# A hand-made order for three engines, a sum made by an accumulating transfer, and one more seven-product step per chunk, in a macaron FFN layer

## The chip, the cores and the metric

The kernel runs on one core of a Trainium2 chip. The metric is the time of one execution on the device, in microseconds (us). Five engines work beside each other, each through its own queue and in the order of that queue: TensorE (PE: matmuls, and PEld, its weight loads), VectorE (DVE), ScalarE (ACT), GpSimd (POOL) and SyncE (SP). SP and POOL issue the transfers between DRAM and the on-chip memory SBUF; 16 DMA engines move them. PE writes its results into PSUM.

## The reference

One decoder layer over 256 tokens with a model width of 2048, all in float32:

```python
h = h + 0.5 * swiglu(rmsnorm(h, ffn1_norm[l]), ffn1_w_in[l], ffn1_w_out[l])
u = rmsnorm(h, mix_norm[l]) @ w_in_mix[l]
y_pool = pool_mixer(...)      # trailing-window means, a small matrix per group
y_gla = gla_mixer(...)        # chunked gated linear attention
h = h + concatenate([y_pool, y_gla]) @ w_out_mix[l]
h = h + 0.5 * swiglu(rmsnorm(h, ffn2_norm[l]), ffn2_w_in[l], ffn2_w_out[l])
return rmsnorm(h, final_norm)

def swiglu(h, w_in, w_out):
    gu = h @ w_in
    gate, up = gu[..., :D_FF], gu[..., D_FF:]     # D_FF = 5632
    return (silu(gate) * up) @ w_out
```

The two FFNs (called f and z in the names) take most of the work; the change touches them and only in passing the mixer between them.

## The kernel before

**Matmuls.** Each float32 operand is split into a high part, rounded to the type fp32r, and a low part, the rest (`split_to`, `parts_of`: ACT casts to the high part, L155; DVE subtracts for the low part, L156). One product is three matmuls, high by high, high by low and low by high (`three`, L191).

**Steps.** An FFN runs over 11 chunks of 512 hidden units. For chunk c its *first product* multiplies the 256 tokens with 1024 columns (512 of the gate, 512 of the other half), in 8 steps of 256 rows of the input; a *second product* multiplies the hidden values of two chunks with 1024 output columns, in 4 steps. A step's weights are one raw tile of 1 MB: four blocks of 128 x 512, two rows by two columns, loaded by two DMAs of 512 KB on SP's queue (`load`, L135). The tokens are two blocks as well, so a step is a 2 x 2 by 2 x 2 block product.

An S step (`s_step`, `Group.s`) does it with eight products, 24 matmuls, and needs the parts of the four blocks. A W step (`w_step`, `Group.w`) does it with seven, 21 matmuls, after Winograd: besides three of the blocks it needs four sums of blocks, which DVE makes in the raw tile (L179, three instructions over 2, 1 and 1 blocks), and their parts, so the parts of seven blocks. The left factors' sums (`s_factors`) are made once per FFN. The products of W steps that belong to more than one quarter of the result gather in PSUM tiles of their own (pw); after the last W step of a chunk `combine` adds them up (an ACT copy, L297, and four DVE sums, L298 to L301) into the two tiles add, and at the chunk's end two DVE additions (L483) bring them to the rest (ps).

A chunk's string in `KINDS` says which steps are W. From chunk 3 on it is WWWWWWSS.

**Chunk end.** Each half of the 256 tokens has its silu on ACT (L490) and its gate product on DVE (L492), then PE transposes the result in 8 small matmuls (L499), and ACT and DVE split that (L504, L505). The order of groups (`GROUPS`) puts a second product over the two chunks before in between: after chunk c's first product comes the second product of chunks c-2 and c-1 for one half of the output columns. Its result is halved on ACT (L534) and added to h in DRAM by accumulating DMAs on POOL's queue (L537). The last two second products of an FFN end in `finish`.

**Buffers.** A ring of 4 raw tiles (3, and 1 more in the FFNs), and a ring of blocks for the parts: 16, and 6 more in the FFNs, taken round and round.

**Order.** The code is written step by step; the framework's scheduler decides the order of every engine's queue from its own timing estimate, so an engine's instructions of neighbouring steps are mixed. DMAs on SP are issued in the order in which their tiles are taken.

Of the kernel before, what the change touches and what calls it, by code (L numbers as in the profile page):

```python
# [33 lines left out]
ALU = mybir.AluOpType  # L34
# [25 lines left out]
W_PAIRS = (1, 3, 4, 6, 2, 5)  # L60
CHUNKS = ("WWWWWWSS",) * 8
# [11 lines left out]
RING = 16  # L73
MORE_RAW = 1
MORE_RING = 6
WIDE = True
# [6 lines left out]
def layer(ctx: ExitStack, tc: tile.TileContext, io):  # L83
# [35 lines left out]
    raws, blocks = Ring(), Ring()  # L119
# [25 lines left out]
    def parts_of(src, runs, cw=CW):  # L145

        res = []
        for x in runs:
            i = x.start
            while i < x.stop:  # L150
                n, new = blocks.take(x.stop - i)
                hi, lo = (y[:, :, :cw] for y in new)
                for j in range(0, n, 2):
                    k = min(j + 2, n)
                    nc.scalar.copy(out=hi[:, j:k, :], in_=src[:, i + j : i + k, :])  # L155
                nc.vector.tensor_tensor(  # L156
                    out=lo, in0=src[:, i : i + n, :], in1=hi.bitcast(F32), op=ALU.subtract
                )
                res += [(hi[:, j, :], lo[:, j, :]) for j in range(n)]
                i += n  # L160
        return res

# [4 lines left out]
    def s_step(src, parts=1, runs=WIDE):  # L167

        w = load(src, parts=max(parts, 2)).rearrange("p (b c) -> p b c", c=CW)
        b = parts_of(w, SINGLES if parts == 4 else PAIRS if parts == 2 or not WIDE else ALL)  # L170
        return lambda k, n: b[n if k == 0 else 3 - n]

    def w_step(src):

        w = load(src).rearrange("p (b c) -> p b c", c=CW)
        f = dict(zip(("B11", "B22", "B21"), parts_of(w, (slice(0, 1), slice(2, 4)))))

        def less(out, x, y):
            nc.vector.tensor_tensor(out=out, in0=x, in1=y, op=ALU.subtract)  # L179


        less(w[:, 0:2, :], w[:, 1:2, :].broadcast_to([P, 2, CW]), w[:, 0:4:2, :])
        less(w[:, 2, :], w[:, 2, :], w[:, 0, :])
        less(w[:, 3, :], w[:, 3, :], w[:, 2, :])
        f.update(zip(("T1", "T3", "T2", "T4"), parts_of(w, PAIRS)))
        return f
# [6 lines left out]
    class Group:  # L193
# [35 lines left out]
        def s(self, a, block):  # L229
# [7 lines left out]
            for k in range(2):  # L237
                for t in range(NT):
                    for n in range(2):
                        self.part(a, block, t, n, k, self.bound[f"{t}{n}"] == self.n - 1 and k == 1)  # L240

# [18 lines left out]
        def w(self, a, s, b):  # L260

            if self.one is None:
# [6 lines left out]
                first = True  # L269
# [864 lines left out]
```

## Time and profile before

| | |
|---|---|
| three runs | 1703.19, 1703.42, 1704.94 us (median 1703.42) |
| span of the profiled execution | 1702.4 us |
| granted TensorE clock, mean | 0.998 |
| DMA, mean | 215 GB/s; 335.6 MB on SP's queue, 27.3 MB on POOL's |
| FFN f, mixer, FFN z, begin of their first matmul | 5.6, 702.6, 1001.0 us |
| a chunk of FFN z (first product to the next first product) | 62.1 us |

The profiled execution has no time of its own beside its span; the span, from its first to its last instruction, is 1.0 us under the median of the runs. In the rows of the profile a line number (L191) is a line of the kernel, x is a count, and a tile's name is that of the program without its number: ps_fi is the sum of FFN f's first product (input), ps_fo its second product (output), pw_fi the extra products of its W steps; zi and zo are the same for FFN z. Raw tiles and blocks taken from the FFNs' own part of the rings are called fring and zring, the others ring. In the view of the windows each row has the stretch, its length, and for PE, PEld, DVE, ACT and POOL the busy time with the number of instructions, then the granted clock, the share of DMA time and GB/s.

### The profile page before, as it was taken

To read this page: it belongs to the slowest core of one execution; us is meant where nothing else is said; L and a number is where in the kernel's file an instruction comes from. 1 tells how busy PE (TensorE), PEld (TensorE's weight loads), DVE (VectorE), ACT (ScalarE), POOL (GpSimd) and SP (SyncE) were. 2 spreads that over 40 slices of the span, in tenths; PEclk is the share of its full clock that TensorE was granted. 3 is DMA by queue.
4 is the path that set the end of the run, shared out by engine and by line. 5 is a ranking of instruction groups with operands and counts; after the bars stand their busy time and mean duration, and the time that the engine had idled before them with its cause. 6 is when DMAs were issued, how large, how long until landed. Compare 5 with 4: busy or idle time off the path is not lost.

```text
span 1702.4 us, 20984 instructions
## 1 busy us (share of the span) xinstructions
PE 1689.7 (99%) x7705; PEld 1403.1 (82%) x7705; DVE 1411.5 (83%) x1565; ACT 999.3 (59%) x1272; POOL 62.9 (4%) x70
## 2 busy tenths in 40 slices
PE   9999999999999999999999999999999999999997
PEld 7888888888888888888988888888888888888886
DVE  8779999999999996645564677999999999998974
ACT  7655666665666664563454554666656656566553
POOL 0000000000000000000000000000000000000012
PEclk9999999999999999999999999999999999999999
DMA  9856856857767776554665764676666667677781
GB/s 355 338 142 229 259 156 229 269 165 221 259 178 221 246 240 215 185 182 139 197 214 169 228 203 155 196 249 195 214 244 208 203 235 227 192 245 218 215 298 50
DMA packets 105241, 365.30 MB, mean 215 GB/s; under 512 B 11809, under 2 KB 15009, under 8 KB 105138
## 3 DMA queue, kind: packets, MB, share of 16 engines
q1 hardware_dynamic: 97026, 335.63, 58.1%
q0 software_dynamic: 7392, 27.27, 8.1%
q8 instruction: 60, 0.98, 0.2%
q10 hardware_dynamic: 720, 1.07, 0.2%
q14 instruction: 43, 0.35, 0.1%
HBM read 338.75 MB, written 25.17 MB: 214 GB/s over the span
## 4 chain that ended last, share of the span: by engine, by line
PE 91%; DVE 5%; DMA 2%; issue 1%; ACT 1%; SPq 0%; POOL 0%; POOLq 0%; ACTq 0%; DVEq 0%
PE ps_fi L191 17%; PE ps_zi L191 14%; PE ps_fo L191 14%; PE ps_zo L191 12%; PE pw_fi L191 8%; PE pw_zi L191 7%; PE ps_h L191 5%; PE ps_mp L191 3%; PE ps_mv L191 3%; DVE ring_lo L156 2%; PE ps_mg L191 2%; PE ps_mq L191 1%; DMA ring_raw<-in_ffn_w_out 1%; PE ps_w_mk L191 1%; DVE ring_raw L179 1%
## 5 line engine op out<-in xcount | busy, mean ns | idle before, releaser
L155 ACT CAST ring_hi<-ring_raw 128x1024 fp32r<-128x1024 f32 (+3 forms) x544 | 501.4, 942 | 381.6 <-DMA ring_raw<-in_ffn_w_in 79.8
L156 DVE TENSOR_TENSOR ring_lo<-ring_raw,ring_hi 128x1024 fp32r<-128x1024 f32 (+6 forms) x463 | 573.8, 1250 | 182.5 <-ACT ring_hi L155 181.4
L179 DVE TENSOR_TENSOR ring_raw<-ring_raw 128x512 f32<-128x512 f32 (+1 forms) x243 | 207.4, 862 | 0.3
L155 ACT CAST zring_hi<-ring_raw 128x1024 fp32r<-128x1024 f32 (+1 forms) x113 | 99.6, 887 | 54.5 <-DMA ring_raw<-in_ffn_w_out 11.8
L191 PE MATMUL ps_fi<-ring_lo,xT_hi 128*128 128x512 f32 x324 | 126.5, 390 | 0.5 <-DVE ring_lo L156 0.4
L191 PE MATMUL ps_fi<-ring_hi,xT_lo 128*128 128x512 f32 x324 | 125.8, 389 | 0.0
L191 PE MATMUL ps_fi<-ring_hi,xT_hi 128*128 128x512 f32 x324 | 124.2, 390 | 1.2 <-ACT ring_hi L155 1.2
L156 DVE TENSOR_TENSOR zring_lo<-ring_raw,zring_hi 128x1024 fp32r<-128x1024 f32 (+3 forms) x101 | 112.2, 1117 | 11.9 <-ACT zring_hi L155 11.8
L155 ACT CAST ring_hi<-zring_raw 128x1024 fp32r<-128x1024 f32 (+1 forms) x85 | 84.2, 991 | 48.0 <-PE ps_zi L191 22.8
L191 PE MATMUL ps_zi<-ring_lo,h_hi 128*128 128x512 f32 x288 | 112.1, 389 | 0.0
L191 PE MATMUL ps_zi<-ring_hi,h_lo 128*128 128x512 f32 x288 | 112.1, 390 | 0.0
L191 PE MATMUL ps_zi<-ring_hi,h_hi 128*128 128x512 f32 x288 | 111.3, 390 | 0.0
L156 DVE TENSOR_TENSOR ring_lo<-zring_raw,ring_hi 128x1024 fp32r<-128x1024 f32 (+2 forms) x65 | 94.2, 1451 | 7.4 <-ACT ring_hi L155 7.3
L191 PE MATMUL ps_fo<-ring_lo,fhi 128*128 128x512 f32 x240 | 93.9, 391 | 0.0
L191 PE MATMUL ps_fo<-ring_hi,flo 128*128 128x512 f32 x240 | 93.8, 391 | 0.0
L191 PE MATMUL ps_fo<-ring_hi,fhi 128*128 128x512 f32 x240 | 93.4, 391 | 0.0
L191 PE MATMUL pw_zi<-ring_hi,s_z 128*128 128x512 f32 x262 | 92.5, 389 | 0.0
L191 PE MATMUL ps_zo<-ring_lo,zhi 128*128 128x512 f32 x234 | 91.5, 391 | 0.0
L191 PE MATMUL ps_zo<-ring_hi,zlo 128*128 128x512 f32 x234 | 91.4, 391 | 0.0
L191 PE MATMUL ps_zo<-ring_hi,zhi 128*128 128x512 f32 x234 | 90.7, 390 | 0.0
L191 PE MATMUL pw_fi<-ring_hi,s_f 128*128 128x512 f32 x226 | 78.7, 389 | 0.0
L155 ACT CAST ring_hi<-fring_raw 128x512 fp32r<-128x512 f32 (+1 forms) x69 | 56.9, 832 | 33.6 <-DVE fring_raw L179 9.8
(324 smaller groups left out, 3730.5 us busy)
## 6 DMA issues: line engine op xcount, KB each, us to landing
ring_raw<-in_ffn_w_in SPq DMA_DIRECT2D x262, 512.0 KB, 5.6
ring_raw<-in_ffn_w_out SPq DMA_DIRECT2D x136, 512.0 KB, 5.2
fring_raw<-in_ffn_w_in SPq DMA_DIRECT2D x44, 512.0 KB, 5.5
zring_raw<-in_ffn_w_in SPq DMA_DIRECT2D x44, 512.0 KB, 4.3
ring_raw<-in_w_out_mix SPq DMA_DIRECT2D x32, 512.0 KB, 4.3
fring_raw<-in_ffn_w_out SPq DMA_DIRECT2D x20, 512.0 KB, 6.0
zring_raw<-in_ffn_w_out SPq DMA_DIRECT2D x20, 512.0 KB, 6.0
hd<-half_f POOLq DMA_DIRECT2D x18, 512.0 KB, 8.1
```

The source lines that it names most:

```text
L155: nc.scalar.copy(out=hi[:, j:k, :], in_=src[:, i + j : i + k, :])
L156: nc.vector.tensor_tensor(out=lo, in0=src[:, i : i + n, :], in1=hi.bitcast(F32), op=ALU.subtract)
L179: nc.vector.tensor_tensor(out=out, in0=x, in1=y, op=ALU.subtract)
L191: nc.tensor.matmul(ps, x, y, start=start and i == 0, stop=stop and i == 2, **kw)
```

## The change

1. **One more W step.** The string of chunks 3 to 10 becomes SWWWWWWW: seven W steps, and the S step comes first. A seventh left factor is made in each FFN's chunk 0.
2. **A sum by a transfer.** The blocks of a step are packed in another order, and the Winograd sums take other signs, so that the first of them is the sum of two blocks. It isn't made by DVE: a DMA of 256 KB on POOL's queue reads the second block again from DRAM and adds it onto the first in the raw tile (`accum_op`), after the load. DVE makes the three others in two instructions (L279, over 1 and 2 blocks).
3. **Order by hand.** From chunk 1 of each FFN up to its last but one second product, DVE, ACT and PE issue in the order of the code (`tc.manual_schedule`). `middle` writes that order: the preparation of a step is cut into phases (casts of its blocks, their low parts, the sums, casts and low parts of the sums), each taken as far ahead as blocks are free; the matmuls of a step come in two units; the chunk's additions and gates follow one unit after the chunk's last, its transposes two units later.
4. **Blocks.** The ring of parts becomes 15 blocks and 6 more, given out by `Blocks`: in `middle` 9 of them in runs of three for the blocks of W steps, 12 for all else, the longest unused first.

The core of the diff:

```diff
-W_PAIRS = (1, 3, 4, 6, 2, 5)
-CHUNKS = ("WWWWWWSS",) * 8
+W_PAIRS = (1, 3, 4, 6, 2, 5, 0)
+CHUNKS = ("SWWWWWWW",) * 8
-RING = 16
+RING = 15
+GATE_AT = 1
+TURN_AT = 2
+T_BLOCKS = 12
+STRIDE = {"t": 2, "b": 3}
+IN_ORDER = {mybir.EngineType.DVE, mybir.EngineType.Activation, mybir.EngineType.PE}
...
-        less(w[:, 0:2, :], w[:, 1:2, :].broadcast_to([P, 2, CW]), w[:, 0:4:2, :])
-        less(w[:, 2, :], w[:, 2, :], w[:, 0, :])
-        less(w[:, 3, :], w[:, 3, :], w[:, 2, :])
...
+        def need(self, phase):
+            w = self.kind == "W"
+            return {"hi_b": ("b", 3) if w else ("t", 4), "hi_t": ("t", 4 if w else 0)}.get(phase)
...
+            w = load(self.src).rearrange("p (b c) -> p b c", c=CW)
+            self.raw = w
+            self.parts = {"b": w[:, 1:4, :], "u": w[:, 0:4:2, :], "t": w[:, 1:4:2, :]}
...
+            if self.kind == "W":
+                nc.gpsimd.dma_start(
+                    out=self.raw[:, 0, :], in_=self.src[:, CW : 2 * CW], accum_op=ALU.add
+                )
...
+            tt(w[:, 2, :], w[:, 0, :], w[:, 2, :], ALU.subtract)
+            tt(w[:, 1:4:2, :], w[:, 1:4:2, :], w[:, 2:3, :].broadcast_to([P, 2, CW]), ALU.subtract)
...
-            nc.vector.tensor_tensor(out=c[:, 1, :], in0=p75[:, 1, :], in1=u2, op=ALU.add)
+            nc.vector.tensor_tensor(out=c[:, 1, :], in0=p75[:, 1, :], in1=u2, op=ALU.subtract)
...
+            for k in range(-1, len(steps)):
+                phases += [("hi_b", k + 1), ("lo_b", k), ("sums", k), ("hi_t", k), ("lo_t", k)]
...
+            def prepare(upto):
+                nonlocal at
+                while at < len(phases):
+                    phase, k = phases[at]
+                    need = steps[k].need(phase)
+                    if need and need[1] > blocks.room(need[0]):
+                        break
+                    getattr(steps[k], phase)()
+                    at += 1
+                assert at > upto
...
+        opening(0)
+        with tc.manual_schedule(engines=IN_ORDER):
+            grp = middle(GROUPS[1:-1])
...
-        b = np.stack([b[:, :, :, 0, 0], b[:, :, :, 0, 1], b[:, :, :, 1, 1], b[:, :, :, 1, 0]], 3)
+        b = np.stack([b[:, :, :, 0, 1], b[:, :, :, 0, 0], b[:, :, :, 1, 1], b[:, :, :, 1, 0]], 3)
```

Three places show the new order. First VectorE's queue within a run of W steps of FFN f, before (L156 is a low part, L179 a difference of blocks):

```order
L179 TENSOR_TENSOR ring_raw<-ring_raw 128x1024
L156 TENSOR_TENSOR ring_lo<-ring_raw,ring_hi 128x1024
L179 TENSOR_TENSOR fring_raw<-fring_raw 128x1024
L156 TENSOR_TENSOR ring_lo<-ring_raw,ring_hi 128x1024 x2
L179 TENSOR_TENSOR ring_raw<-ring_raw 128x512
L156 TENSOR_TENSOR ring_lo<-ring_raw,ring_hi 128x1024 x2
L179 TENSOR_TENSOR ring_raw<-ring_raw 128x512 x2
```

And of the change (L220 is a low part, L279 a difference), two W steps:

```order
L220 TENSOR_TENSOR fring_lo<-fring_raw,fring_hi 128x1536
L279 TENSOR_TENSOR fring_raw<-fring_raw 128x512
L279 TENSOR_TENSOR fring_raw<-fring_raw 128x2x512
L220 TENSOR_TENSOR ring_lo<-fring_raw,ring_hi 128x1024 x2
L220 TENSOR_TENSOR fring_lo<-ring_raw,fring_hi 128x1536
L279 TENSOR_TENSOR ring_raw<-ring_raw 128x512
L279 TENSOR_TENSOR ring_raw<-ring_raw 128x2x512
L220 TENSOR_TENSOR ring_lo<-ring_raw,ring_hi 128x1024 x2
```

Steps that were mixed now follow one another whole, with each difference right behind what it waits for. Second, VectorE's queue at the end of chunk 4 of FFN f, of the change (fi in the names is the first product; L440 to L443 are the four sums of `combine`, L628 the two additions, L637 the gates, L654 the transposed chunk's low parts):

```order
L442 TENSOR_TENSOR add_fi_1_1985<-pw_fi_1_1771,add_fi_1_1985 128x512
L443 TENSOR_TENSOR add_fi_1_1985<-pw_fi_1_1771,add_fi_1_1985 128x512
L220 TENSOR_TENSOR ring_lo<-fring_raw,ring_hi 128x2048
L628 TENSOR_TENSOR ps_fi_0_1740<-ps_fi_0_1740,add_fi_0_1984 128x1024
L628 TENSOR_TENSOR ps_fi_1_1741<-ps_fi_1_1741,add_fi_1_1985 128x1024
L637 SCALAR_TENSOR_TENSOR fa_0_2014<-ps_fi_0_1740,rx_r,fs_0_2012 128x512
L637 SCALAR_TENSOR_TENSOR fa_1_2018<-ps_fi_1_1741,rx_r,fs_1_2016 128x512
L220 TENSOR_TENSOR ring_lo<-ring_raw,ring_hi 128x2048
L654 TENSOR_TENSOR flo_2059<-ftp_2049,fhi_2058 128x4x128 x2
L220 TENSOR_TENSOR ring_lo<-ring_raw,ring_hi 128x2048 x2
```

Before, some ten other instructions of later steps stood among these; now one low part stands between the sums and the additions, and nothing between additions and gates. Third, TensorE's queue at the same chunk end, of the change (ps_fo is the second product that follows chunk 4, ftp the transposed chunk):

```order
L303 MATMUL ps_fo_2_1_1992<-ring_lo,fhi_1216 128x512
L303 MATMUL ps_fo_2_1_1992<-ring_hi,flo_1217 128x512
L648 MATMUL ftp_2049<-ident,fa_0_2014 128x128 x4
L648 MATMUL ftp_2049<-ident,fa_1_2018 128x128 x4
L303 MATMUL ps_fo_2_0_1991<-ring_hi,fhi_1216 128x512
L303 MATMUL ps_fo_2_0_1991<-ring_lo,fhi_1216 128x512
```

The first product of chunk 4 has 171 matmuls where it had 174, and the eight transposes stand together behind 36 matmuls of the second product; before, the two halves stood apart, four behind 48 and four behind 52. On POOL's queue the 126 accumulating transfers into raw tiles stand in the order of their steps; those of a chunk's first four W steps are ahead of the two transfers that put the second product before them away.

330 lines of the change are left out of this document (237 added, 93 removed).

## The prediction

> **What bounds the kernel now.** The page first: its busy times, and the slices of VectorE.
>
> ```profile
> span 1702.4 us, 20984 instructions
> PE 1689.7 (99%) x7705; PEld 1403.1 (82%) x7705; DVE 1411.5 (83%) x1565; ACT 999.3 (59%) x1272; POOL 62.9 (4%) x70
> DVE  8779999999999996645564677999999999998974
> ```
>
> TensorE (PE) is busy 99% of the span, but VectorE (DVE) stands at nine tenths or more in the FFN stages, so both have to be followed. Second, the view of the waits, for PE alone:
>
> ```profile
> PE idle L575 <- DVE zeros L570: 1.2, 1, 1.2
> PE ps_fi L191 <- ACT ring_hi L155: 1.2, 2, 0.8
> PE ps_fi L191 <- DVE ring_lo L156: 0.4, 2, 0.2
> ```
>
> 2.8 us of waits in all, at the start and once later. A busy PE may still be a slow one, so third, its order of time within a run of seven-product steps, and two windows:
>
> ```profile
> 299.64 0.39 PE L191 MATMUL pw_fi<-ring_hi,xT_hi 128*128 128x512 f32 x1
> ...
> 311.88 0.39 PE L191 MATMUL pw_fi<-ring_lo,s_f 128*128 128x512 f32 x1
> ```
>
> ```profile
> 1161.88:1201.32 39.44, 39.44 (x175) 32.66 (x174) 35.20 (x36) 24.63 (x28) 0.85 (x1) 1.00 0.77 230
> 1223.98:1286.15 62.17, 62.17 (x280) 51.47 (x278) 59.61 (x62) 38.85 (x47) 1.71 (x2) 1.00 0.69 220
> ```
>
> Between the two rows quoted lie 54 starts, so a matmul starts every 12.24 / 54 = 0.2267 us, though its row says 0.39 (its result is late by the difference). The first window is one chunk's first product: 174 matmuls in 39.44 us, again 0.2267. So PE runs back to back, and a matmul that goes is 0.2267 us, if it stays fed. The second window is a whole chunk: 62.17 us, of which DVE works 59.61. The other engine is 96% full there.
>
> **What the change takes from PE.** The order shows 174 matmuls becoming 171 in chunks 3 to 10 of both FFNs (one eight-product step of 24 becomes one of 21); all other counts stay. 16 x 3 = 48 matmuls x 0.2267 = **10.9 us**. A chunk has 171 + 96 matmuls and 8 transposes: 62.17 - 0.68 = 61.5 us.
>
> **What it does to DVE.** The groups by form and the spacing of DVE's and ACT's own instructions:
>
> ```profile
> L155 ACT CAST ring_hi<-ring_raw 128x1024 fp32r<-128x1024 f32 x403 | 415.7, 1050 | 254.5 <-DVE ring_raw L179 27.3 <-PE ps_fi L191 26.9 <-DMA ring_raw<-in_ffn_w_out 26.4
> L156 DVE TENSOR_TENSOR ring_lo<-ring_raw,ring_hi 128x1024 fp32r<-128x1024 f32 x256 | 310.1, 1221 | 106.6 <-ACT ring_hi L155 105.9
> L156 DVE TENSOR_TENSOR ring_lo<-ring_raw,ring_hi 128x2048 fp32r<-128x2048 f32 x66 | 151.1, 2291 | 36.7 <-ACT ring_hi L155 36.7
> L179 DVE TENSOR_TENSOR ring_raw<-ring_raw 128x512 f32<-128x512 f32 x162 | 110.5, 684 | 0.2
> L179 DVE TENSOR_TENSOR ring_raw<-ring_raw 128x1024 f32<-128x1024 f32 x81 | 98.6, 1218 | 0.1
> L156 DVE TENSOR_TENSOR ring_lo<-ring_raw,ring_hi 128x1536 fp32r<-128x1536 f32 x15 | 26.3, 1750 | 6.8 <-ACT ring_hi L155 6.8
> L483 DVE TENSOR_TENSOR ps_fi<-ps_fi,add_fi 128x1024 f32<-128x1024 f32 x18 | 22.1, 1225 | 0.0
> L492 DVE SCALAR_TENSOR_TENSOR fa<-ps_fi,rx_r,fs 128x512 f32<-128x512 f32 x22 | 16.3, 743 | 0.0
> L490 ACT ACTIVATE fs<-ps_fi,rx_r 128x512 f32<-128x512 f32 x22 | 15.0, 686 | 13.4 <-DVE ps_fi L483 11.5 <-PE ps_fi L191 1.7
> ```
>
> ```profile
> 1174.54 1.21 DVE L156 TENSOR_TENSOR ring_lo<-ring_raw,ring_hi 128x1024 fp32r<-128x1024 f32 x1
> 1175.67 1.21 DVE L156 TENSOR_TENSOR zring_lo<-ring_raw,zring_hi 128x1024 fp32r<-128x1024 f32 x1
> ```
>
> ```profile
> 1174.64 1.05 ACT L155 CAST ring_hi<-zring_raw 128x1024 fp32r<-128x1024 f32 x1
> 1175.60 0.61 ACT L155 CAST ring_hi<-ring_raw 128x512 fp32r<-128x512 f32 x1
> ```
>
> ```profile
> 49.49 0.29 DVE L385 TENSOR_TENSOR sf_f<-sf_f,sa_f 128x128 f32<-128x128 f32 x1
> 49.81 0.29 DVE L385 TENSOR_TENSOR sf_f<-sa_f,sf_f 128x128 f32<-128x128 f32 x1
> ```
>
> Independent neighbours on DVE start 1.13 apart where one lasts 1.21: the next one starts 0.08 early. ACT's casts start 0.09 early. A neighbour that needs the other's result starts 0.03 after its end (49.49 + 0.29 to 49.81). So 512, 1024, 1536 and 2048 columns occupy DVE for 0.60, 1.14, 1.67 and 2.21 us, and a dependent instruction sees them after 0.71, 1.25, 1.78 and 2.32.
>
> A seven-product step before: lower parts of 1, 2, 2 and 2 blocks, differences of 2, 1 and 1: 0.60 + 3 x 1.14 + 1.14 + 2 x 0.60 = 6.36 us. After: 1.67 + 2 x 1.14 for the lower parts, 0.60 + 1.14 for the differences: 5.69. A chunk before: 6 x 6.36 + 6 x 2.21; after: 7 x 5.69 + 5 x 2.21. That is 51.4 against 50.9, beside the same chunk end. So the accumulating transfer pays for the seventh step: DVE's share of a chunk stays about the same, (59.61 - 0.5) / 61.5 = 96%. By shares PE remains the bound.
>
> **What the order by hand does.** Shares hide that DVE, ACT and PE now each follow one fixed order. Before, six steps with seven products come first and two with eight last, so that the four L298-L301 sums have 48 matmuls of cover before the chunk's end; the transposes follow 20 to 55 matmuls after it. Now the chunk ends with its last seven-product step, the sums, two additions and two gates come behind it, and the transposes stand after exactly 36 matmuls. I walk the longest chain. Casts of step k+1's three blocks stand on ACT ahead of step k's second casts, and need the blocks of step k-2. So from the moment PE is done with the first 9 matmuls of the chunk's first seven-product step:
>
> - casts for the fourth step (0.19 for PE's late result, 0.96 + 0.53), then the third step's cast (1.08) and two lower parts (2 x 1.14): 5.0 us
> - steps four to seven: 1.78 + 0.71 + 1.25 + 1.08 + 1.14 = 5.96 each (the cast waits for the second difference, the last lower part for the cast): 23.8
> - the next step's lower part in halves (2.28), the four sums (2.62, two of them waiting for the one before), another lower part (2.21), two additions (1.14 + 1.25), the second activation (0.72) and gate (0.77): 11.0
>
> Sum 39.9 us. PE has in the same stretch 12 + 6 x 21 + 36 = 174 matmuls and four transposes (0.35, a chunk's eight taking some 0.7): 39.4 + 0.35 = 39.8 us. **It is a tie**, short by 0.1, and forty intervals read to 0.01 make that uncertain by some 0.3. Where the chain is longer than PE's work, PE waits at the transposes by the difference, once in each of 16 chunks. Below nothing it cannot go: PE has no idle time to give back but the 2.8 us. I take 0.2 us a chunk, 3 us; the ends are 0 and 0.5 (8 us).
>
> **The accumulating transfers.** 126 of 256 KB are added, on POOL's queue, each behind its step's load and ahead of the first difference. What stands for them:
>
> ```profile
> ring_raw<-in_ffn_w_in SPq DMA_DIRECT2D x262, 512.0 KB, 5.6
> hd<-half_f POOLq DMA_DIRECT2D x18, 512.0 KB, 8.1
> q1 hardware_dynamic: 97026, 335.63, 58.1%
> q0 software_dynamic: 7392, 27.27, 8.1%
> ```
>
> ```profile
> L537 POOL DMA_DIRECT2D hd<-half_f x18: 853/862/1006, 107.7 to 607.5; - x18
> DMA to landing us min/median/max: 5.4/7.9/11.3
> ```
>
> The accumulating transfers of before (512 KB into DRAM) land in 5.4 to 11.3 us, 7.9 in the median. At half the size I take 6, from 4 to 8. When is one late? A chunk has 4 raw tiles, so a step's load waits for the lower parts of the step four ahead. Within a run that is 3 x 5.96 + 1.78 = 19.7 us before the difference, against 5.6 + 6. The tight one is the chunk's first seven-product step, whose raw tile is freed by the second step of the product before. The walk begins 138 matmuls, 31.3 us, before the chunk's end; 28.9 us later, 2.4 before that end, DVE takes up the halves (2.28), the sums (2.62) and that second lower part (2.32): free 4.8 us after the end. Additions and gates bring DVE to 8.4, then come a lower part (2.21), the transposed chunk's two lower parts with a wait for ACT (1.9), two lower parts (4.4) and the step's own (1.78): its difference is due at 18.7. Of the 13.9 us between, the load takes 5.6: a landing of the sum up to **8.3 us** costs nothing. The second such step has the same room. Behind the accumulate on POOL's queue stand the two put-away transfers of the group, needed a chunk later. Transfer time: bytes on the software queue cost 8.1% / 27.27 MB against 58.1% / 335.63 MB, 1.7 times as much; seven of 0.26 MB add some 9.3 us of 16 engines to a chunk's 0.69 x 62.2 = 43: 0.85 of the time. Loads will land later, but most have 5 us of room.
>
> POOL writes these transfers' descriptors beside a full DVE:
>
> ```profile
> 1163.40 0.85 POOL L537 DMA_DIRECT2D hd<-half_z  x1 [1.87 <-ACT half_z L534]
> ...
> 1163.94 1.22 DVE L179 TENSOR_TENSOR zring_raw<-zring_raw 128x1024 f32<-128x1024 f32 x1
> ```
>
> Neither is longer than its group's mean, so I charge nothing. The Trainium skill (SBUF — State Buffer, "Summary: rules for kernel authors") warns against hiding such a transfer under a DVE instruction, since DVE in its two-port modes locks the descriptor writer out; by that rule sums would land late, as in the rival below. The same page of the Trainium skill ("Who interferes with whom") has no two-port mode for this DVE instruction, and the rows agree. The Trainium skill's fit for one such transfer (DMA: Bandwidth & Descriptors, "Anatomy of one DMA") would give, as an estimate, 2.6 us for 256 KB; by it no sum would ever be late.
>
> **Other edits**, at nothing: a seventh set of left factors in the opening chunk, where DVE's slices stand at 7 to 9 tenths and PE has its work ahead; a ring of 15 blocks instead of 16, in stages where DVE is at 4 to 6 tenths; new signs in the sums. If the cover fails, each is under 1 us, once per FFN.
>
> **The sum.** 1702.4 - 10.9 + 3 = 1694.5 us of span. The median of the three runs, 1703.42, lies 1.0 above the span; with that, **1695.5 us**.
>
> **Rivals.**
> - *The chain is longer than I read.* 0.5 to 1 us in each of 16 chunks: 8 to 16 us back, 1700.5 to 1708.5. For it: the tie, and DVE at 96%. Against: every interval is from rows. Chance 0.18.
> - *The sum lands late* (slower). From a landing of 8.3 us on, each further microsecond moves the whole chain behind it; the gain of 0.68 a chunk is gone at 9.0. At 10.5 us it costs 2.2 x 16 = 35: 1703.4 - 10.9 + 35 = 1727.5; at the 11.3 of the slowest row, 1740.5. For it: the row's upper half, and more traffic. Against: half the bytes, and no write to DRAM. Chance 0.17.
> - *It doesn't feed less at all*: no stall anywhere, 1692.5. It is within the forecast's own spread.
>
> **How the numbers follow.** Forecast (stalls of 0 to 0.5 us a chunk: 1692 to 1700.5) 0.65; longer chain 0.18; late sums 0.17. The range runs from 1691.5 to 1710, over the first two, leaving the last out. A measurement here tells 0.2%, 3.4 us, from no change: faster (below 1700) 0.64, within (to 1706.8) 0.15, slower 0.21.
>
> **What would show it.** PE's waits: under 10 us in all, on DVE at the transposes, is the forecast; 1 us at each chunk's transposes is the first rival; DVE waiting on the accumulating transfer at the first difference of a chunk, and PE behind it, the second. The chunk's length should be 61.5 to 62.0 us, matmuls 0.2267 apart, 48 fewer of them, DMA near 0.85. A landing over 8.3 us, or DVE intervals longer than read beside the added transfers, would make me wrong.

## The result, and the profile after

The changed kernel takes **1724.79 us** (median of four runs, 1723.97 to 1726.89), the kernel before 1703.48 beside it: a ratio of 1.0126, with an interval of 1.0112 to 1.0141. It is 1.3% slower. The forecast was 1695.5, 0.5% faster. First the head of the page of after:

```profile
span 1725.1 us, 21190 instructions
PE 1686.3 (98%) x7657; PEld 1394.0 (81%) x7657; DVE 1428.5 (83%) x1353; ACT 1011.7 (59%) x1231; POOL 174.6 (10%) x196
```

TensorE has its 48 matmuls less (7705 to 7657) and VectorE's share has not changed. So the work came out as planned and the time is in waits. TensorE's waits of after (the engine's line, whom it waited for, us in all, times, the longest):

```profile
PE ps_zo L303 <- DVE add_zi L440: 9.6, 8, 1.7
PE ps_fo L303 <- DVE add_fi L440: 9.0, 8, 1.3
PE pw_zi L303 <- DVE ring_lo L220: 2.5, 4, 1.2
...
PE pw_fi L303 <- DVE ring_lo L220: 1.8, 4, 0.8
PE pw_zi L303 <- DVE zlo L654: 1.6, 1, 1.6
```

Before, all waits together were 2.8 us. Now the first matmul of the second product (ps_fo, ps_zo) waits in each of the 16 late chunks for L440, the first of the four sums that close the seven-product steps: 18.6 us. It doesn't read that sum. It writes the PSUM tile that the sum is the last to read: with two sets of two PSUM tiles used in turn, a second product accumulates where the extra products (pw) of the first product before it stood. One such place, first on TensorE, then on VectorE (start, duration, and in brackets the wait):

```profile
526.13 0.39 PE L303 MATMUL ps_fi<-ring_hi,xT_lo 128*128 128x512 f32 x1
527.79 0.50 PE L303 MATMUL ps_fo<-ring_hi,fhi 128*128 128x512 f32 x1 [1.27 <-DVE add_fi L440]
528.13 0.39 PE L303 MATMUL ps_fo<-ring_lo,fhi 128*128 128x512 f32 x1
```

```profile
522.45 4.69 DVE L220 TENSOR_TENSOR ring_lo<-ring_raw,ring_hi 128x1024 fp32r<-128x1024 f32 x4
527.06 0.68 DVE L440 TENSOR_TENSOR add_fi<-pw_fi,add_fi 128x512 f32<-128x512 f32 x1
```

The chunk's last matmul starts at 526.13, the next could start at 526.36, and L440 ends at 527.74: it stands behind four lower parts, two of the chunk's last seven-product step and two of the second product's first step. TensorE loses more than the 1.27 us that are put down to the wait: it starts 1.43 late, and its next start follows after 0.34 us instead of 0.23, some 1.54 in all.

A second thing shows on VectorE: it waits for the accumulating transfers. The row of its waits:

```profile
DVE ring_raw L279 <- DMA ring_raw<-in_ffn_w_in: 18.4, 11, 2.6
```

One such place in the order of time, on VectorE, then on SyncE and POOL, which issue the load and the sum:

```profile
472.01 2.28 DVE L220 TENSOR_TENSOR ring_lo<-ring_raw,ring_hi 128x2048 fp32r<-128x2048 f32 x1
...
486.67 1.75 DVE L220 TENSOR_TENSOR fring_lo<-ring_raw,fring_hi 128x1536 fp32r<-128x1536 f32 x1
490.27 1.95 DVE L279 TENSOR_TENSOR ring_raw<-ring_raw 128x512 f32<-128x512 f32 x2 [1.86 <-DMA ring_raw<-in_ffn_w_in]
```

```profile
474.36 7.12 SPq L185 DMA_DIRECT2D ring_raw<-in_ffn_w_in  x6
```

```profile
481.05 0.86 POOL L265 DMA_DIRECT2D ring_raw<-in_ffn_w_in  x1 [7.11 <-DVE ring_lo L220]
```

This is a chunk's second seven-product step. Its raw tile comes free at 474.29, with the first row, a lower part of the second product's third step. The load is issued at 474.36 (the first of three in that row), the sum at 481.05, and by VectorE's start the sum has landed at some 490.24, 9.2 us after its issue; VectorE was ready for it at 488.41. (The bracket of POOL's row names the lower part that freed the tile. That had ended long before; in the code the sum stands behind its load, so the load is the likelier last.) Eleven of the 16 late chunks have such a wait, of 0.76 to 2.56 us, all at this step, with the sum issued 8.6 to 9.9 us before VectorE's start. At the end of these chunks TensorE waits 1.00 to 1.65 us for L440, in the other five 0.89 or 0.90 and once 1.17. So the late sums add to a wait that is there without them. Over all 126 such transfers, by the view of their line, the landing is this:

```profile
DMA to landing us min/median/max: 4.1/6.9/13.5
```

One chunk from end to end, and its VectorE work beside it (window, length, busy us of PE, PEld, DVE, ACT and POOL, granted clock, DMA share):

```profile
486.86:550.62 63.76, 62.04 (x276) 50.78 (x275) 60.33 (x52) 39.51 (x46) 7.89 (x9) 1.00 0.84 244
```

The DMA share of 0.84 is as forecast (0.85). VectorE's 60.3 us are 1.2 more than the forecast's 59.1 (59.61 less 0.5), and the chunk takes 63.8 us where 61.5 to 62.0 were forecast.

### The profile page after: what moved, and what is told of

Its sections match the earlier page's. It is cut to its first block, busy times and chain, and to the rows that moved or that the text cites. A ratio compares the mean times of both kernels' runs of the same rounds, so it can differ in the third digit from the quotient of the medians.

```text
span 1725.1 us, 21190 instructions
## 1 busy us (share of the span) xinstructions
PE 1686.3 (98%) x7657; PEld 1394.0 (81%) x7657; DVE 1428.5 (83%) x1353; ACT 1011.7 (59%) x1231; POOL 174.6 (10%) x196
## 5 line engine op out<-in xcount | busy, mean ns | idle before, releaser
L217 ACT CAST ring_hi<-ring_raw 128x1024 fp32r<-128x1024 f32 (+3 forms) x558 | 552.4, 1014 | 379.8 <-issue 78.3
L220 DVE TENSOR_TENSOR ring_lo<-ring_raw,ring_hi 128x1024 fp32r<-128x1024 f32 (+5 forms) x443 | 633.7, 1446 | 156.2 <-ACT ring_hi L217 153.6
L279 DVE TENSOR_TENSOR ring_raw<-ring_raw 128x512 f32<-128x512 f32 (+1 forms) x178 | 170.6, 959 | 24.1 <-DMA ring_raw<-in_ffn_w_in 18.4
L303 PE MATMUL ps_fo<-ring_hi,fhi 128*128 128x512 f32 x352 | 138.8, 395 | 9.0 <-DVE add_fi L440 9.0
L265 POOL DMA_DIRECT2D ring_raw<-in_ffn_w_in x89 | 77.1, 866 | 695.8 <-DMA ring_raw<-in_ffn_w_in 349.7
L303 PE MATMUL ps_zo<-ring_hi,zhi 128*128 128x512 f32 x344 | 135.6, 395 | 9.6 <-DVE add_zi L440 9.6
L303 PE MATMUL ps_fo<-ring_hi,flo 128*128 128x512 f32 x352 | 137.2, 390 | 0.0
L303 PE MATMUL pw_fi<-ring_hi,s_f 128*128 128x512 f32 x366 | 122.8, 389 | 0.0
L217 ACT CAST ring_hi<-zring_raw 128x1024 fp32r<-128x1024 f32 x82 | 80.2, 1003 | 38.8 <-DVE zring_raw L279 23.4
L220 DVE TENSOR_TENSOR ring_lo<-zring_raw,ring_hi 128x1024 fp32r<-128x1024 f32 (+2 forms) x60 | 91.8, 1539 | 6.3 <-ACT ring_hi L217 6.2
L217 ACT CAST ring_hi<-fring_raw 128x1024 fp32r<-128x1024 f32 x72 | 71.5, 1015 | 35.2 <-issue 13.4
L220 DVE TENSOR_TENSOR ring_lo<-fring_raw,ring_hi 128x1024 fp32r<-128x1024 f32 (+2 forms) x54 | 81.4, 1518 | 12.2 <-ACT ring_hi L217 11.7
```

The source lines that it names most:

```text
L217: nc.scalar.copy(out=hi[:, j:k, :], in_=src[:, j:k, :])
L220: nc.vector.tensor_tensor(out=lo, in0=src, in1=hi.bitcast(F32), op=ALU.subtract)
L265: nc.gpsimd.dma_start(out=self.raw[:, 0, :], in_=self.src[:, CW : 2 * CW], accum_op=ALU.add)
L279: nc.vector.tensor_tensor(out=out, in0=x, in1=y, op=op)
L303: nc.tensor.matmul(ps, x, y, start=start and i == 0, stop=stop and i == 2, **kw)
```

## The experiments

All times are medians, each ratio is to the kernel before on the same chip, whose medians there were 1702.96 to 1703.60 us.

| run | us | ratio to before, interval |
|---|---|---|
| eight-product step last (s_last) | 1706.72 | 1.0021, 1.0012 to 1.0031 |
| four sums ahead of two lower parts (sums_first) | 1764.20 | 1.0354, 1.0339 to 1.0369 |
| no accumulating transfers (no_sum) | 1713.92 | 1.0059, 1.0044 to 1.0074 |
| six seven-product steps (six_w) | 1704.70 | 1.0008, 0.9998 to 1.0018 |
| s_last, lower part in halves, one step moved (best_a) | 1705.73 | 1.0013, 1.0005 to 1.0022 |
| only the first sum ahead (sums_split) | 1783.39 | 1.0463, 1.0447 to 1.0479 |
| s_last, VectorE makes the sum (dve_sum_s) | 1773.97 | 1.0412, 1.0398 to 1.0427 |
| before with seven such steps (before7) | 1806.38 | 1.0605, 1.0589 to 1.0621 |
| ScalarE frees the tile (act_frees) | 1722.44 | 1.0110, 1.0095 to 1.0124 |
| best_a, one copy earlier (best_b) | 1703.80 | 1.0004, 0.9995 to 1.0013 |
| s_last without transfers (no_sum_s) | 1705.71 | 1.0012, 1.0003 to 1.0022 |
| best_b, shorter chain (best_c) | 1693.95 | 0.9950, 0.9937 to 0.9962 |
| changed kernel, shorter chain (chain_short) | 1718.67 | 1.0100, 1.0078 to 1.0121 |
| no transfers, ScalarE frees the tile (tile_no_sum) | 1704.80 | 1.0008, 0.9999 to 1.0017 |

### The eight-product step last

```diff
-CHUNKS = ("SWWWWWWW",) * 8
+CHUNKS = ("WWWWWWWS",) * 8
```

> The eight-product step of chunks 3 to 10 stands last in the chunk (WWWWWWWS) instead of first; nothing else changes, so matmuls, vector work and transfers keep their numbers. Theory (TensorE waits at the second product's first matmul for the PSUM tile that the first of the four sums at L440 frees, and the last seven-product step at the chunk's end leaves no matmuls to cover that): 24 matmuls, 5.4 us, now stand between; the 16 waits on L440 (18.6 us of idle time) go, the waits on the seventh step's lower parts (4.3 us) stay or double, and the time is 1700 to 1706 us. Rival (VectorE's chain as a whole is too long, or the accumulating sums land late): the waits only move, to the seventh step's lower parts or to the transposes, 15 us or more of them remain, and the time is 1715 to 1726.

1706.7 us, 18 less than the changed kernel with the same work, just above what the theory gave. TensorE's waits:

```profile
PE ps_zi L303 <- DVE ring_lo L220: 2.5, 8, 0.4
PE ps_fi L303 <- DVE ring_lo L220: 2.4, 8, 0.4
PE pw_zi L303 <- DVE zlo L654: 1.6, 1, 1.6
```

No wait on L440 is left. But 16 small ones have come, 0.3 us each, on the lower part of the eight-product step: VectorE comes out of the seven steps a little late here too. So the place of that step is worth 18 us, though this run can't say whether it is the tile or something that comes with it.

### Six seven-product steps in the new order

```diff
-CHUNKS = ("SWWWWWWW",) * 8
+CHUNKS = ("WWWWWWSS",) * 8
```

> All of the change but the seventh seven-product step: chunks are WWWWWWSS as before, with the accumulating transfers and the order by hand. 48 matmuls come back (10.9 us). Theory: 48 matmuls (10.9 us) stand between the four sums and the second product, and the chain through six steps is shorter than TensorE's work, so TensorE waits under 5 us in all; 1702 to 1706 us, the time of the kernel before. Rival (the order by hand or the 126 transfers cost by themselves): 1710 to 1725, with waits of TensorE over 10 us.

1704.7: the theory. TensorE's waits are 4.7 us in all, and the ratio's interval holds 1. So the order by hand and the transfers (110 with six such steps, not the 126 of the expectation) cost nothing measurable by themselves; what the changed kernel loses comes with the seventh step and its place.

### The four sums ahead of the next lower parts

```diff
-                    prepare(place["lo_t" if i and steps[k].kind == "W" else "lo_b", k])
+                    prepare(
+                        place["lo_t" if i and steps[k].kind == "W" else "lo_b", k],
+                        not (steps[k].kind == "W" and steps[k + 1].kind == "S"),
+                    )
```

(The new argument stops `prepare` at the phase that is asked for, so the next step's lower parts are written behind L443, and two of ScalarE's casts behind its copy at L439.)

> The order of chunks stays SWWWWWWW; on VectorE the four sums at L440 to L443 are moved ahead of the two half lower parts of the second product's first step (2.3 us). Theory (the PSUM wait is real, but VectorE is also late with everything else at this place): the waits on L440 go, and TensorE waits instead for the lower parts behind the sums, 1.5 to 2.2 us a chunk; 1722 to 1737 us. Rival (only the place of the sums in VectorE's order was wrong): TensorE does not wait there at all, 1702 to 1707.

1764.2, beyond both. The direction is the theory's, the size is not:

```profile
PE ps_zo L303 <- DVE ring_lo L220: 19.4, 8, 2.8
PE ps_fo L303 <- DVE ring_lo L220: 19.0, 8, 2.4
```

The waits on L440 are gone, and TensorE waits 2.4 us in each chunk for the half lower parts that now stand behind four sums of 0.7. VectorE has nothing to spare there: what is moved ahead of one wait is paid at the next. Part of the size is another thing. Behind the stop that ends at 541.78 the granted clock (the last but two of the row) was 0.52 for 3.5 us:

```profile
541.78:545.25 3.47, 3.47 (x8) 2.76 (x9) 3.47 (x3) 0.00 (x0) 0.00 (x0) 0.52 0.60 209
```

TensorE's matmuls start 0.43 us apart there, not 0.23. Behind an equally long stop, which ends at 607.43, the clock was 1.00. The two kinds come about in turn, and chunks of the first take 65.7 us, of the second 64.1. So this time is not the price of VectorE's order alone. The second try in this direction moved only the first sum ahead:

```diff
             nc.vector.tensor_tensor(out=u2, in0=p16[:, 1, :], in1=c[:, 0, :], op=ALU.add)
+
+        def combine_rest(self):
...
+                    if rest:
+                        rest.pop()()
```

> The order of chunks is SWWWWWWW; on VectorE only the first of the four sums stands ahead of the two half lower parts of the second product's first step, the other three behind them. Theory (TensorE waits for that one sum, since it alone frees the first PSUM tile, and the first half lower part can be ready 0.7 us later): the waits on the first sum go, those on the half lower parts stay under 0.5 us a chunk; 1702 to 1712 us. Rival (VectorE's whole chain is the bound in this order, as the 1764 us with all four sums ahead suggest): TensorE waits at the lower parts or at the transposes instead, over 1720.

1783.4, with 47.8 us of waits on lower parts of the second product. The time says little, since the edit also moved the next 2048-column lower part behind the additions and gates. TensorE's order of time takes the waits apart, here at one chunk's end:

```profile
545.63 0.50 PE L303 MATMUL ps_fo<-ring_lo,fhi 128*128 128x512 f32 x1 [0.27 <-DVE ring_lo L220]
...
554.67 0.50 PE L303 MATMUL ps_fo<-ring_lo,fhi 128*128 128x512 f32 x1 [2.70 <-DVE ring_lo L220]
```

The wait on the first sum is gone, the half lower part costs 0.27 us, as the theory had it, and the last sum (L452, at 548.69) 0.26. The 2.70 are for the 2048-column lower part that the edit moved, which ends at 554.62. So the rows bear out what the theory said of the first sum and the half lower parts; what this order would take without the other move was not run.

### Without the accumulating transfers

```diff
-            if self.kind == "W":
-                nc.gpsimd.dma_start(
-                    out=self.raw[:, 0, :], in_=self.src[:, CW : 2 * CW], accum_op=ALU.add
-                )
```

> The changed kernel without its 126 accumulating transfers: the sum that they make is left out of the computation, nothing else changes. Theory (the order of VectorE against the PSUM tiles costs the time): the 16 waits on L440 stay near 1 us each; VectorE loses its 18 us of waits on these transfers, of which TensorE gets back less than half; 1712 to 1724 us. Rival (the sums land late and push the whole chain): the waits of TensorE on L440 and on lower parts fall below 6 us in all, 1694 to 1703.

1713.9, 10.9 below the changed kernel, in the theory's range. TensorE's waits:

```profile
PE ps_zo L299 <- DVE add_zi L436: 7.8, 8, 1.6
PE ps_fo L299 <- DVE add_fi L436: 7.1, 8, 0.9
```

The waits on the first sum (L436 here) stay, 14.9 us in 16 chunks, 0.88 to 0.90 in all but the last, as in the changed kernel's chunks without a late sum; and those on the seventh step's lower parts are gone. So the transfers cost the changed kernel some 11 us, more than the "less than half" of VectorE's 18 us that the theory allowed; and the wait at the first sum is there without any late transfer. The same edit where the eight-product step is last:

> The kernel with the eight-product step last, without its 126 accumulating transfers: the sum that they make is left out of the computation. It gives the price of the transfers where the PSUM tile is covered. Theory (there VectorE runs back to back through the seven steps, and the sums land in time): 1702 to 1706.5 us, at most 4 us below the kernel with them. Rival (late landings or the slower loads cost as much here as the 11 us that they cost in the changed kernel): 1694 to 1698.

1705.7 against 1706.7: 1 us, within what the runs can tell. There (in s_last) VectorE waited for a sum only three times, 1.7 us in all, with the 16 DMA engines as full (0.87 in a chunk). So the added traffic by itself is not what costs the 11 us. Late sums are thus a matter of that order too: with four raw tiles a load takes over the tile of the step four ahead. With the eight-product step first that is, for the second seven-product step, the second product's third step; with it last it is the second product's second, whose lower part VectorE makes ahead of the additions and gates. (That this is what brings the sums in time follows from the order and was not tried by itself.)

### ScalarE frees the PSUM tile

```diff
             nc.scalar.copy(out=c[:, 0, :], in_=p16[:, 0, :])
-            nc.vector.tensor_tensor(out=u2, in0=p16[:, 1, :], in1=c[:, 0, :], op=ALU.add)
+            nc.scalar.copy(out=u2, in_=p16[:, 1, :])
+            nc.vector.tensor_tensor(out=u2, in0=u2, in1=c[:, 0, :], op=ALU.add)
```

> The changed kernel (SWWWWWWW) with one edit: ScalarE copies the second half of the PSUM tile too, 512 columns, 0.57 us, so that the first of the four sums reads two copies in SBUF and the tile is free when ScalarE is done, not when VectorE has worked through the four lower parts ahead of that sum. VectorE's order and work stay. Theory (that tile is what TensorE waits for): the 16 waits on the first sum become waits on ScalarE's copy of 0.3 us or less; since VectorE is no earlier, part of the gain comes back as waits on the second tile's sums or on lower parts; 1708 to 1718 us. Rival (VectorE's chain is the bound of the whole chunk, the tile only the place where it shows): all of it comes back, 1720 to 1727.

1722.4, the rival. The first sum frees nothing any more and TensorE doesn't wait for it, yet only 2.4 us are won by the medians, with the two kernels' runs overlapping (1718.8 to 1724.8 against 1724.0 to 1726.9):

```profile
PE pw_zi L303 <- DVE ring_lo L220: 5.3, 7, 1.1
PE pw_fi L303 <- DVE ring_lo L220: 3.4, 7, 0.8
PE ps_zo L303 <- DVE add_zi L444: 3.3, 8, 1.0
PE ps_fo L303 <- DVE add_fi L444: 2.7, 8, 0.4
```

The time came back as waits on the seventh step's lower parts and on L444, the last sum, which frees the second tile. Both edits together:

> The changed kernel without its accumulating transfers (that sum is left out of the computation) and with ScalarE's second copy, so that ScalarE frees the first PSUM tile: the two edits together that gave 1713.9 (no transfers) and 1722.4 us (the copy) alone. Theory (two causes: VectorE enters the chain late by the late sums, and the tile waits for VectorE's place; with the sums gone the seventh step's lower parts are in time, so that freeing the tile now pays): the waits on the first sum, 0.89 us in each chunk, shrink to some 0.3 us on the second tile's last sum; 1703 to 1709 us. Rival (VectorE's chain is the bound in any case): the waits come back elsewhere, 1711 to 1715.

1704.8, the theory. With the sums out of the way freeing the tile is worth 9.1 us (1713.9 to 1704.8); with them in, 2.4. TensorE's waits on the last sum (L440 here) remain, 4.8 us in 16 chunks:

```profile
PE ps_zo L299 <- DVE add_zi L440: 2.7, 8, 0.8
PE ps_fo L299 <- DVE add_fi L440: 2.1, 8, 0.3
```

So there are two causes in a row: in most chunks a late sum makes VectorE enter the last steps late, and even a punctual VectorE reaches the first sum 0.9 us after TensorE wants its tile.

### The price of the seventh step without the transfer

The kernel before with WWWWWWWS, its own order and its own differences:

```diff
-W_PAIRS = (1, 3, 4, 6, 2, 5)
-CHUNKS = ("WWWWWWSS",) * 8
+W_PAIRS = (1, 3, 4, 6, 2, 5, 0)
+CHUNKS = ("WWWWWWWS",) * 8
-RING = 16
+RING = 15
```

> The kernel before with only the seventh seven-product step (WWWWWWWS), its own order of instructions and its own differences on VectorE, and a ring of 15 blocks instead of 16 to make room for the seventh set of left factors. Theory (a seven-product step costs VectorE 6.36 us without the transfer, so a chunk's VectorE work is 59.6 + 4.2 = 63.8 us against 61.5 of TensorE): about 2 us a chunk over, 1720 to 1745 us. Rival (the seventh step is to be had without the transfer and the order by hand): 1691 to 1700.

1806.4: the theory's direction at more than three times its size. In a window of 66 us VectorE has only 58.5 us of work, so the sum of its instructions, on which the expectation rested, doesn't give the time here; TensorE's waits are spread over VectorE, ScalarE and five tiles, and were not followed further.

```profile
500.00:566.00 66.00, 61.05 (x254) 47.30 (x253) 58.53 (x64) 36.43 (x45) 1.73 (x2) 0.97 0.66 199
```

And s_last without the transfers and with VectorE making the sum:

```diff
+            tt(w[:, 0, :], w[:, 0, :], w[:, 1, :], ALU.add)
             tt(w[:, 2, :], w[:, 0, :], w[:, 2, :], ALU.subtract)
```

> The kernel with the eight-product step last, the sum of each seven-product step made by VectorE (one more 512-column addition, 0.70 us, ahead of the first difference) instead of the accumulating transfer. Theory (VectorE's chain through seven such steps ties with TensorE's work, so that each addition lengthens it): 7 x 0.6 to 0.7 us a chunk, 16 chunks, less what is idle now: 1750 to 1785 us. Rival (VectorE has room, the transfer was not needed): 1700 to 1715.

1774.0, the theory: 67 us above s_last, 4.2 per chunk, for seven additions. The transfer does pay for the seventh step.

### Toward a better order, and the chain itself

From s_last on, the next wait each time:

```diff
-                        (Step(kind, w_in[g, kp]), a_of(kp), kp if kind == "W" else None)
-                        for kind, kp in pairs_of(g)
+                        (
+                            Step(kind, w_in[g, kp], kind == "S" and i == 7 and g > 2),
+                            a_of(kp), kp if kind == "W" else None,
+                        )
+                        for i, (kind, kp) in enumerate(pairs_of(g))
...
-    "z": ("SSSSSSSS", "SWSWWWSS", "WWSWWWSS") + CHUNKS,
+    "z": ("SSSSSSSS", "SSWWWWSS", "WWSWWWSS") + CHUNKS,
```

> The kernel with the eight-product step last, with two more edits: the lower part of that last step is made in two halves (in chunks 3 to 10), and the second chunk of the second FFN has its first seven-product step one place later (SSWWWWSS instead of SWSWWWSS). Theory (what the kernel with the eight-product step last still loses is its 16 waits on that lower part, gaps of some 0.45 us each, and the one wait on the transposed chunk's lower part, 1.8 us): both go, 1706.7 - 7.2 - 1.8 = 1697.7, say 1696 to 1700 us, below the kernel before. Rival (VectorE is late with everything behind): the waits move to the transposes or to the next lower parts, 1703 to 1708.

1705.7, the rival: 1 us won, within what the runs can tell. The 16 waits went, and TensorE waited for ScalarE's put-away copy instead, at the other end of the same PSUM tile's life:

```profile
PE pw_zi L303 <- ACT half_z L682: 3.0, 6, 0.6
PE pw_fi L303 <- ACT half_f L682: 2.9, 6, 0.6
```

Then that copy was moved ahead of two casts (`prepare` gets the same argument as above):

```diff
+                        i > 0 or behind is None,
```

> The kernel with the eight-product step last, its lower part in halves and the one step moved in the second FFN's second chunk, with one more edit: ScalarE's put-away copy of the second product's first row tile stands ahead of the two casts that wait for TensorE, instead of behind them. There TensorE waited 0.25 to 0.62 us in 12 of 16 chunks (the first PSUM tile of the next chunk's extra products is the one that this copy reads). Theory (a chunk has 61.5 us of TensorE work and VectorE some 60.3, so with both waits on PSUM tiles covered TensorE is the bound): these 12 gaps of 0.6 us go, 1705.7 - 7 = 1698.7, say 1697 to 1701 us. Rival (VectorE's chain from the first seven-product step to the last eight-product one is longer than TensorE's work by some 0.4 us a chunk): the wait comes back at the next place, 1703 to 1707.

1703.8, the rival again, and no different from before. The waits moved a third time, to VectorE's lower parts of the seventh step:

```profile
PE pw_zi L303 <- DVE ring_lo L220: 3.5, 8, 0.8
PE pw_fi L303 <- DVE ring_lo L220: 2.9, 7, 0.4
```

Three places in turn with the same loss: not a place but the chain through them is too long. So the next edit touched neither tile nor place, only the chain. The next step's three-block lower part goes between a step's two differences, so that no instruction waits for the result of the one just ahead:

```diff
+                ahead = 0 <= k < len(steps) - 1 and steps[k].kind == steps[k + 1].kind == "W"
-                phases += [("hi_b", k + 1), ("lo_b", k), ("sums", k), ("hi_t", k), ("lo_t", k)]
+                phases += [("hi_b", k + 1), ("lo_b", k), ("sum1", k)]
+                phases += [("lo_b", k + 1)] if ahead else []
+                phases += [("sum2", k), ("hi_t", k), ("lo_t", k)]
```

> The last kernel (eight-product step last, three edits on orders) with VectorE's order within a run of seven-product steps changed: the next step's lower part of three blocks stands between a step's two differences instead of behind its other lower parts. Same work; two starts per step that waited for the result of the instruction just ahead no longer do (0.12 us each by the rows of before). The pitch of such a step on VectorE falls from 6.05 to some 5.82 us, 0.9 us or more over the four steps of the chain that ends at the seventh step's lower parts, where TensorE waited 15 times by some 0.44 us (gaps of 0.62). Theory (that chain is what TensorE waits for): these waits go, 1703.8 - 9 = 1694.8, say 1693 to 1698 us. Rival (the wait comes back at another place, or the step's own lower parts, 1.67 us later now, come too late): 1701 to 1706.

1693.95, the theory, 0.5% below the kernel before. VectorE's order of time in best_b, then in best_c, one step each:

```profile
504.29 1.95 DVE L279 TENSOR_TENSOR fring_raw<-fring_raw 128x512 f32<-128x512 f32 x2
...
510.36 1.95 DVE L279 TENSOR_TENSOR ring_raw<-ring_raw 128x512 f32<-128x512 f32 x2
```

```profile
486.55 0.68 DVE L285 TENSOR_TENSOR ring_raw<-ring_raw 128x512 f32<-128x512 f32 x1
487.15 1.75 DVE L220 TENSOR_TENSOR fring_lo<-ring_raw,fring_hi 128x1536 fp32r<-128x1536 f32 x1
488.82 1.22 DVE L285 TENSOR_TENSOR ring_raw<-ring_raw 128x1024 f32<-128x1024 f32 x1
489.96 2.48 DVE L220 TENSOR_TENSOR ring_lo<-ring_raw,ring_hi 128x1024 fp32r<-128x1024 f32 x2
492.36 0.69 DVE L285 TENSOR_TENSOR ring_raw<-ring_raw 128x512 f32<-128x512 f32 x1
```

A step takes 6.07 us in the one and 5.81 in the other: 0.26 for two starts that no longer wait. TensorE's waits are then:

```profile
PE ztp L656 <- DVE za L645: 2.1, 2, 1.9
PE idle L812 <- DVE zeros L807: 1.2, 1, 1.2
PE ps_fi L311 <- ACT ring_hi L217: 0.7, 2, 0.4
PE ps_fi L311 <- DVE ring_lo L220: 0.2, 1, 0.2
```

None is left in the late chunks. The same edit alone on the changed kernel:

> The changed kernel (SWWWWWWW) with the same shortened order within the runs of seven-product steps and nothing else. VectorE's work, the PSUM tiles and the transfers are as in the changed kernel. Theory (the chain on VectorE through the seven steps, entered late where a sum lands late, decides; the PSUM tile is only the first place where it meets TensorE): 0.9 to 1.4 us of each chunk's 1.2 us wait on the first sum and 0.3 us on lower parts come back; 1703 to 1713 us. Rival (the place of the sums behind four lower parts decides): 1718 to 1726.

1718.7 (1715.2 to 1724.6): 6 us won by the medians, though the runs overlap; that is less than the theory had, and at the low end of the rival's range. The waits on the first sum (L448 here) fall from 18.6 to 9.6 us, and VectorE still waits for late sums:

```profile
PE ps_zo L311 <- DVE add_zi L448: 5.0, 8, 1.4
PE ps_fo L311 <- DVE add_fi L448: 4.6, 8, 0.9
```

```profile
DVE ring_raw L285 <- DMA ring_raw<-in_ffn_w_in: 13.9, 12, 1.6
```

The profiled execution (1716.7 us, one of the faster) shows where the theory holds. From each chunk's first transpose to the next, the 16 late chunks take 1000.2 us in all, 1014.3 in the changed kernel's and 982.9 in best_c's: 14 us won and 17 still lost. But the first two such stretches of the second FFN take 104.6 us where they took 100.3; the wait on the transposed chunk's lower part there is 3.2 us instead of 1.6. So in that order of chunks the chain's length is a part of the loss, not the whole.

## Why the prediction was wrong, point by point

- **TensorE's saving** (48 matmuls, 10.9 us) was right: 7705 to 7657, and best_c, where the waits of the late chunks are gone, is 9.6 us under the kernel before.
- **VectorE's share** (about the same, since the transfer pays for the seventh step) was right in the main; dve_sum_s shows the price without it. But 60.3 us in a chunk are 1.2 more than its sum gave. That sum let every instruction start 0.08 us before the end of the one ahead, and the two differences of a step, in the fixed order, cannot. In best_c, with the same work and these waits gone, a chunk has 59.4.
- **The walk is the step that failed.** It compared VectorE's chain with TensorE's work at one place, the transposes, 36 matmuls into the second product, and took 0.2 us a chunk there. It never asked what the second product's first matmul waits for, and so put the wait for the PSUM tile at nothing. By its own numbers the chain is late there: 28.9 + 2.28 + 0.71 = 31.9 us to the end of the first sum, where TensorE has 138 matmuls, 31.3 us. That is 0.6 us a chunk at the PSUM tile. The 36 matmuls on which the walk counted are not cover for it, they stand behind it. In no_sum the walk can be followed, from the cast that waits for TensorE to the first sum:

```profile
1236.68 1.05 ACT L217 CAST zring_hi<-ring_raw 128x1024 fp32r<-128x1024 f32 x1 [3.10 <-PE pw_zi L299]
1265.76 2.35 DVE L220 TENSOR_TENSOR ring_lo<-ring_raw,ring_hi 128x1024 fp32r<-128x1024 f32 x2
1268.03 0.68 DVE L436 TENSOR_TENSOR add_zi<-pw_zi,add_zi 128x512 f32<-128x512 f32 x1
```

  From that cast to the halves at 1265.76 are 29.1 us, where the walk has 28.7 (28.9 without its first 0.19); the sum ends at 1268.71, and TensorE, whose last matmul before started at 1267.49, could have gone on at 1267.72.
- **The pitch** of a step was read as 5.96 us and is 6.07 (the rows of best_b); four of them make 0.4 us. With the 0.6 this is 1.0 a chunk, as in the rows above; the waits put down to it without the transfers are 14.9 us in 16 chunks, 0.93.
- **The late sums** were a rival (1727.5, chance 0.17), put aside because a landing up to 8.3 us was to cost nothing, the load taking 5.6 of 13.9 us, with "the same room" at the second step. In the case above the sum was issued 6.7 us after the load, and landed 9.2 us later: 15.9 us, where VectorE needed it after 14.1. It was late by 1.8. The rival's mechanism was right, at the second such step rather than the first, at 11 us for the whole kernel rather than 35. Landings were taken as 6 us. They were 6.9 in the median of all 126, but 8.6 to 9.9 in the 11 places where VectorE waited, with the 16 DMA engines 0.93 full in the case above: a busy place, which the median doesn't show, and a slower load. The Trainium skill's fit for one transfer on this queue (DMA: Bandwidth & Descriptors, "Anatomy of one DMA"), 2.6 us as an estimate for this size, does not hold for these sums beside this kernel's loads: the shortest landing was 4.1.
- **Issue cost on POOL** at nothing held: VectorE's commonest group, by form, takes 1224 ns in the mean, 1221 before.

```profile
L220 DVE TENSOR_TENSOR ring_lo<-ring_raw,ring_hi 128x1024 fp32r<-128x1024 f32 x300 | 363.1, 1224 | 93.9 <-ACT ring_hi L217 91.5
```

- **Other edits at nothing** weren't tried one by one; six_w has them all, at 1704.7. What the prediction didn't walk at all is the order by hand outside the late chunks: the second FFN's second chunk has one wait on the transposed chunk's lower part (L654, 1.6 us), in the changed kernel, in s_last and in six_w, and none before.
- **The sum**: the forecast without its 3 us of stalls was 1692.5, and the changed kernel is 32.3 us above that. Of these 10.9 are the transfers (no_sum), 9.1 more the tile (tile_no_sum), and 12.3 are left in tile_no_sum. There the 16 late chunks take 993.2 us, 10.3 more than in best_c, where TensorE doesn't stop in them: 4.8 are recorded as waits on the last sum, and some 0.3 more go with each of the 16 stops. The wait at L654 is 1.6, and 0.4 are left over. The causes overlap, so their order matters: in the changed kernel the tile alone gives 2.4 and the chain alone 6, by the medians.

## What to carry to other kernels

When a chain on one engine ties with another engine's work, compare them at every point where the second takes something from the first, buffers that it must get back included, not only at the end of the chain; the earliest such point with no work ahead of it decides. A wait that changes its place from edit to edit at the same cost is the sign of a chain that is too long: shorten the chain, by putting independent work between dependent instructions, before moving its ends. For a transfer that follows another, count the two landings together, and take what a landing lasts beside the traffic of that place, not the median of all.

## What the runs showed of the hardware

- A 256 KB accumulating transfer into the on-chip memory, beside the loads of this kernel, landed in 4.1 to 13.5 us, 6.9 in the median. The accumulating put-aways of 512 KB beside them went from 5.4/7.9/11.3 us (least, median, most) to 7.4/10.3/14.3.
- Two starts on VectorE that no longer depend on the instruction just ahead made a step of 6.07 us one of 5.81; over 16 chunks of seven steps, on a path where TensorE waited, that was 9.9 us of the kernel (1703.8 to 1693.95) at the same work.
- A stop of TensorE cost more than the wait that the profile puts down to it. The 16 late chunks took 982.9 us without stops (best_c), 993.2 with waits of 4.8 us in them (tile_no_sum) and 1002.7 with 14.9 (no_sum): some 0.3 us more for each stop.
- After stops of 2.37 us the granted clock was 0.52 for 3.5 us at one place and 1.00 at another (sums_first, 541.78 and 607.43). No run here shows what decides between them.
